# RWKV7 heads in a two-block kernel: one stationary tile of 128 columns for a chunk's outputs and next state, transposes in place of identity products, masked products in another order

## The chip, the cores and the metric

The kernel runs on one core of one Trainium2 chip. The metric is the device time of one execution in microseconds. A core has a tensor array (TensorE, PE in the rows; its weight loads are PEld), VectorE (DVE), ScalarE (ACT), GpSimd (POOL) and SyncE (SP), which issues the loads of the weights. Each engine takes its instructions in the order in which the program has them, and engines wait for one another by semaphores.

## What is computed

Two blocks on 256 tokens of 2048 features. The first has two layers; in each, four mixers of 512 columns (retention, HGRN2, mLSTM, RWKV7) run on one projection, then an output projection and a feed-forward part. The second block is one layer with sparse attention and a dilated mixture. The change lies in RWKV7 of the first block:

```python
def rwkv7_scan(r, log_w, k, v, kk, a):
    def step(state, inp):                      # state: 64 x 64 of each of 8 heads
        rt, lwt, kt, vt, kkt, at = inp
        state = (state * jnp.exp(lwt)[:, :, None, :]
                 - jnp.einsum('bhvk,bhk->bhv', state, kkt)[..., None] * (at * kkt)[:, :, None, :]
                 + vt[..., None] * kt[:, :, None, :])
        return state, jnp.einsum('bhvk,bhk->bhv', state, rt)

def rwkv7_group(p, ...):
    r, k, v, wd, ad, gd = split_cols(p + (token_shift(p) - p) * mu, RWKV_SPLIT)
    log_w = -RWKV_DECAY_SCALE * jax.nn.sigmoid(w0 + jnp.tanh(wd) @ w_up)
    a = jax.nn.sigmoid(a0 + ad @ a_up)
    kk = hs(k * k_k); kk = kk / norm(kk)
    k = k * (1.0 + (a - 1.0) * k_a)
    y = rwkv7_scan(hs(r), hs(log_w), hs(k), hs(v), kk, hs(a))
    ...                                        # norm of each head, bonus, gate
```

## The kernel before

**The stream.** All large matmuls run through `stream_a` (lines 147 to 152) or `stream_b` (195 to 197). A weight tile comes by DMA into `raw` (three buffers), ScalarE casts its high part to `hi` (line 104, four buffers), VectorE subtracts for `lo` (line 105), and the array multiplies both with activations that are split in the same way. A tile of 1024 columns is eight k-tiles; in the jobs of the mixers each k-tile takes three matmuls of 256 columns (lines 147, 148, 149), weights of 128 rows by 128 columns.

**RWKV7.** `rw_pair` handles two heads on 128 partitions, four times in each layer (`rw(0)` to `rw(3)` in `mixers`), so eight times in all. The 256 tokens are four chunks of 64, c = 2e + o. Pairs alternate between two sets of tiles (s = 0, 1) and two banks of PSUM each; `LI` and `TB` are one tile for all. The steps of a pair that matter here:

- line 968: the norm of kappa is spread over rows by two products with the identity (f32 products, two passes each in the trace);
- line 1000: [kappa; beta] x [alpha, rho], of each head the four chunks in a row, one head on partitions 0 to 63, the other on 64 to 127; line 1001 masks them into `W`, which has four slots of 64 columns for each head and chunk;
- lines 1018 to 1027: the inverse of (I + L) of 32 x 32 blocks in four rounds; line 1018 multiplies X with `LI` and, in the same 256 columns, with the identity; ScalarE negates the second half into `TB` (1023), VectorE transposes the first (1020), line 1025 multiplies again, lines 1026 and 1027 put the result into T and X;
- line 1038 transposes [kappa; beta]; lines 1044 and 1045 turn v and alpha by products with the identity, 64 columns of weights each;
- lines 1057 to 1083: the inverse of blocks of 64, X and T [X | alpha];
- line 1090: Ah^T times two slots of W, into two banks `g2[o]`; line 1096 makes `GT` and `PT` of them in four subtractions;
- lines 1103 and 1105: the state at the start of chunks 1 to 3, `W` (128 rows x 64 columns of weights) and `GT` (64 x 64), heads side by side; line 1106 scales it by the decay into `ST`;
- lines 1111 and 1113: the outputs of eight head-chunks from `W` (128 x 64) and `PT` (64 x 64); line 1115 copies them out.

Tile shapes are printed in the rows as rows*columns of weights, such as 64*64.

**What sets the order.** The program is written pair by pair; the tile framework's scheduler lays out each engine's queue by a simulated timeline. `K.first(100)` around `rw_pair` lets its instructions go before the last hundred traced ones, so the matmuls of a pair stand between those of the stream and of HGRN2 (`hg_pair`, lines 800 to 889).

Of the kernel before, what the change touches and what calls it, by code (L numbers as in the profile page):

```python
# [13 lines left out]
OP = mybir.AluOpType  # L14
AX = mybir.AxisListType
PSUM = bass.MemoryType.PSUM

D = 2048
# [10 lines left out]
class Squares:  # L29
    """Tiles of squares yet to be added up, and the bank of their means."""  # L30
# [5 lines left out]
class Core:  # L36
    """Pools, the weight stream and the norms that every part shares."""
# [19 lines left out]
    def g(self, i=0):  # L57
        """One bank of PSUM for the parts beside the stream, from one of their three pools."""
        return self.ps_g[i].tile([128, 512], F32, name="g", tag="g")

    def first(self, n):
        """What is traced in this goes before the n instructions traced last where it can, and beside what follows."""
        return self.tc.high_priority(offset=n)
# [26 lines left out]
    def prep(self, srcs, n, pool=False):  # L90
        """srcs: [128, n] each of DRAM in f32, or all in one [., 128, n] -> the two f32r parts of them all, side by side: hi + lo = w."""
# [16 lines left out]
    def stream_a(self, jobs, rhs, phases, feed=None, late=None, load=None, whole=None, bank=None):  # L108
        """jobs: [(weights [128, K], done, one)]: a tile of 128 columns each; rhs(k): [128, 512] = hi|lo of k-tile k.
        phases: lists of k-tiles (at most 8 in a row); within a phase k is outer over the jobs when there are several.  # L110
        A job with `one` gets the whole sum in its bank, as wide as the half of rhs; else it's the sum of the bank's two halves.
        load(phase), feed(phase): make what rhs gives of the phase; late(): what comes once the last of them are made.
        whole: [jobs, 128, K], the weights of all jobs; bank: where a single job's sum goes."""
# [43 lines left out]
    def stream_n(self, w, rhs, phases):  # L157
        """w: [128, K], only the first 64 of whose tile's 128 columns count; rhs, phases: as for stream_a. Returns their sums [64, 256]:
        the hi parts and the lo parts of the weights go through together."""
# [23 lines left out]
    def stream_b(self, w, nk, lhs, done):  # L183
        """w: [128, nk*512] of DRAM, 512 columns; lhs(k): [128, 512] = hi|lo; done(tt, bank) for the two tiles of tokens."""
# [16 lines left out]
    def half_sum(self, bank):  # L201
        """The two halves of a bank (of x's hi and lo) added, in SBUF."""
# [1880 lines left out]
```

## Time and profile before

| | |
|---|---|
| median of three runs | 3612.31 us (3606.8 to 3613.91) |
| span of the profiled execution, and its own time | 3606.8 us, 3606.8 us |
| tensor array busy (matmuls) | 3520.6 us, 98% |
| VectorE, ScalarE, GpSimd busy | 2484.1, 1746.3, 650.8 us |
| mean granted clock of the array | 0.990 |

The page gives busy time, the chain that ended last and the costliest groups. Matmul records are pipelined, so that the printed length of one overlaps the next; the time that one takes of the array is read from start to start in the timeline. RWKV7's pairs of the first layer lie at 50 to 380 us, those of the second at 1430 to 1780 us.

### The profile page before, as it was taken

Reading aid. Unit: us, or ns where it says so; the run is one execution under the profiler, and the core shown is the slowest. Engines: PE = TensorE matmul, PEld = TensorE weight load, DVE = VectorE, ACT = ScalarE, POOL = GpSimd, SP = SyncE. Lnnn points to the kernel's source line nnn. Section 1 sums busy time; section 2 is a strip of 40 time slices with the busy share of each in tenths; the row PEclk is TensorE's granted clock in tenths of the full one; section 3 lists DMA queues with packets and bytes.
Section 4 is the critical chain, followed back from the end, with each engine's and each line's share of the span. In section 5 each row is a group of like instructions: output and inputs, shape, how many; then the busy total and the mean of one; then the engine's idle time right before and its main releaser. Section 6 shows DMA issues by size and latency. Waiting matters only on the chain.

```text
span 3606.8 us, 62083 instructions
## 1 busy us (share of the span) xinstructions
PE 3520.6 (98%) x23920; PEld 3069.2 (85%) x23920; DVE 2484.1 (69%) x4464; ACT 1746.3 (48%) x2861; POOL 650.8 (18%) x822
## 2 busy tenths in 40 slices
PE   8999999999999999999999899999999999999998
PEld 8778888788888888877888788888888899988886
DVE  7676776777776557876786777777556866765555
ACT  5543454544444444634354544444444644654443
POOL 2122312311110003120420311111002213100001
PEclk9999999999999999999999999999999999999999
DMA  6335555677776664424455577777665555445554
GB/s 205 112 98 162 162 169 164 208 235 235 236 237 215 204 193 154 152 60 139 151 171 180 159 235 236 238 234 232 203 204 154 181 177 175 135 132 186 186 185 141
DMA packets 209369, 652.49 MB, mean 181 GB/s; under 512 B 24176, under 2 KB 27152, under 8 KB 209072
## 3 DMA queue, kind: packets, MB, share of 16 engines
q1 hardware_dynamic: 169664, 577.84, 51.1%
q10 hardware_dynamic: 39408, 70.67, 6.2%
q8 instruction: 188, 3.08, 0.3%
q14 instruction: 109, 0.89, 0.1%
HBM read 645.78 MB, written 2.65 MB: 180 GB/s over the span
## 4 chain that ended last, share of the span: by engine, by line
PE 89%; DVE 6%; issue 2%; ACT 1%; DMA 1%; POOL 0%; SPq 0%; DVEq 0%; ACTq 0%; POOLq 0%
PE s L151 34%; PE s L152 17%; PE s L147 5%; PE s L148 5%; PE s L149 5%; PE s L195 4%; PE s L196 4%; PE s L197 4%; DVE lo L105 1%; DVE h L314 1%; PE g L148 1%; PE g L149 1%; PE g L147 1%; DVE uq L300 1%; PE g L1018 1%
## 5 line engine op out<-in xcount | busy, mean ns | idle before, releaser
L105 DVE TENSOR_TENSOR lo<-raw,hi 128x1024 fp32r<-128x1024 f32 (+1 forms) x1101 | 1383.5, 1258 | 840.3 <-ACT hi L104 835.8
L104 ACT CAST hi<-raw 128x1024 fp32r<-128x1024 f32 (+1 forms) x1105 | 1142.3, 1036 | 1346.9 <-PE s L151 658.7
L151 PE MATMUL s<-uq,hi 128*128 128x512 f32 x3344 | 1176.2, 394 | 3.6 <-ACT hid L211 3.6
L152 PE MATMUL s<-uq,lo 128*128 128x256 f32 x3344 | 933.8, 279 | 0.0
L151 PEld LDWEIGHTS s<-uq,hi 128*128 128x128 f32 x3344 | 627.4, 188 | 154.1 <-ACT hid L211 4.2
L152 PEld LDWEIGHTS s<-uq,lo 128*128 128x128 f32 x3344 | 627.5, 188 | 0.2
L151 PE MATMUL s<-hid,hi 128*128 128x512 f32 x1320 | 466.5, 396 | 0.0
L147 PE MATMUL s<-uq,hi 128*128 128x256 f32 x1456 | 420.0, 288 | 5.1 <-ACT v L1423 4.0
L149 PE MATMUL s<-uq,lo 128*128 128x256 f32 x1456 | 419.4, 288 | 0.0
L148 PE MATMUL s<-uq,hi 128*128 128x256 f32 x1456 | 419.2, 288 | 0.0
L152 PE MATMUL s<-hid,lo 128*128 128x256 f32 x1320 | 372.2, 282 | 0.0
L151 PEld LDWEIGHTS s<-hid,hi 128*128 128x128 f32 x1320 | 248.0, 188 | 60.0
L147 PEld LDWEIGHTS s<-uq,hi 128*128 128x128 f32 x1456 | 276.8, 190 | 14.4 <-issue 6.3
L148 PEld LDWEIGHTS s<-uq,hi 128*128 128x128 f32 x1456 | 276.7, 190 | 7.6 <-issue 6.7
L149 PEld LDWEIGHTS s<-uq,lo 128*128 128x128 f32 x1456 | 276.9, 190 | 7.2 <-issue 6.2
L152 PEld LDWEIGHTS s<-hid,lo 128*128 128x128 f32 x1320 | 247.9, 188 | 0.0
L196 PE MATMUL s<-lo,uq 128*128 128x512 f32 x608 | 243.4, 401 | 2.1 <-DVE lo L105 2.1
L195 PE MATMUL s<-hi,uq 128*128 128x512 f32 x608 | 241.3, 402 | 1.4 <-DVE k L1252 0.7
L197 PE MATMUL s<-hi,uq 128*128 128x512 f32 x608 | 241.9, 400 | 0.0
L223 POOL TENSOR_TENSOR acc<-acc,sq 128x256 f32<-128x256 f32 x70 | 82.9, 1184 | 796.6 <-ACT sq L219 796.6
L373 POOL TENSOR_TENSOR gs<-e,R 128x256 f32<-128x256 f32 x88 | 80.0, 909 | 439.3 <-DVE e L206 404.2
L379 POOL TENSOR_TENSOR e<-e,R 128x256 f32<-128x256 f32 x88 | 79.4, 903 | 367.9 <-DVE e L206 367.9
(638 smaller groups left out, 5259.8 us busy)
## 6 DMA issues: line engine op xcount, KB each, us to landing
raw<-in_wg_dram SPq DMA_DIRECT2D x168, 512.0 KB, 4.6
raw<-in_wu_dram SPq DMA_DIRECT2D x168, 512.0 KB, 4.7
raw<-in_wd_dram SPq DMA_DIRECT2D x160, 512.0 KB, 3.7
raw<-in_wina_dram SPq DMA_DIRECT2D x154, 512.0 KB, 3.9
raw<-in_win2a_dram SPq DMA_DIRECT2D x130, 512.0 KB, 3.7
raw<-in_winb_dram SPq DMA_DIRECT2D x96, 512.0 KB, 3.8
raw<-in_wout_dram SPq DMA_DIRECT2D x96, 512.0 KB, 3.8
aw<-in_wada_dram ACTq DMA_DIRECT2D x192, 256.0 KB, 4.8
```

What stands on the lines that cost most here:

```text
L104: self.last_hi = nc.scalar.copy(hi[:, :n], raw[:, :n])
L105: self.last = (nc.gpsimd if pool else nc.vector).tensor_tensor(lo[:, :n], raw[:, :n], hi[:, :n].bitcast(F32), op=OP.subtract)
L147: nc.tensor.matmul(banks[i][:, 0:n], wh, x[:, 0:n], start=first, stop=False)
L148: nc.tensor.matmul(banks[i][:, 0:n], wh, x[:, n:2 * n], start=False, stop=False)
L149: nc.tensor.matmul(banks[i][:, 0:n], wl, x[:, 0:n], start=False, stop=last)
L151: nc.tensor.matmul(banks[i], wh, x, start=first, stop=False)
L152: nc.tensor.matmul(banks[i][:, 0:256], wl, x[:, 0:256], start=False, stop=last)
L195: nc.tensor.matmul(banks[tt], xh, wh, start=(k == 0), stop=False)
L196: nc.tensor.matmul(banks[tt], xh, wl, start=False, stop=False)
L197: nc.tensor.matmul(banks[tt], xl, wh, start=False, stop=(k == nk - 1))
L223: (nc.vector if i % 2 else nc.gpsimd).tensor_tensor(acc.parts[i % 2], acc.parts[i % 2], sq, op=OP.add)
L373: nc.gpsimd.tensor_tensor(g, e, rget(), op=OP.mult)
```

## The change

- `W` changes its slots: for even chunks [masked alpha | v, alpha | masked rho | kappa, beta], for odd ones the last two are exchanged, so that outputs and next state of a chunk come from one stationary tile of 128 columns, slots 2 and 3 together. The outputs of a chunk then stand on the partitions of its half of a token tile, the state on the others.
- `PG` holds P and G side by side, made in one subtraction from `RI`, a new tile for all pairs with rho and the identity; ScalarE copies rho into it from each pair's `AR`. The eight products of the old line 1090 go to one bank, in the order e, h, o.
- For each chunk two products with `W` (128 rows by 128 columns; 64 columns for the last) and two with `PG` (64 rows) add up in one bank, and one multiplication on 64 partitions makes the next state, with `dcs`, the decays laid out by ScalarE.
- Products with the identity become transposes: of the norm, of v and alpha (four of 128 x 128 instead of eight products with 64 columns), and of X in each round of the inverse.
- The masked products alternate between the heads, on two banks, and are masked in four operations instead of two.
- Docstrings and comments are gone, with blank lines in their place; in `rw_pair` lines move by 4 to 21, after it by 14.

The diff without those docstrings and comments:

```diff
         nc, K = self.nc, self.K
-        self.wLI, self.wTB = self.t([128, 5, 128], "wLI"), self.t([128, 4, 4, 32], "wTB")
-        nc.gpsimd.memset(self.wLI[:, 0:4], 0.0)
+        self.wLI, self.wTB = self.t([128, 4, 128], "wLI"), self.t([128, 4, 4, 32], "wTB")
+        nc.gpsimd.memset(self.wLI, 0.0)
         nc.gpsimd.memset(self.wTB, 0.0)
-        nc.gpsimd.tensor_copy(self.wLI[:, 4], K.ident)
+        self.wRI = self.t([128, 2, 2, 128], "wRI")
+        for o in range(2):
+            Q, i = slice(64 * o, 64 * o + 64), 64 - 64 * o
+            nc.gpsimd.tensor_copy(self.wRI[Q, :, :, i:i + 64].rearrange("p h e t -> p (h e) t"), self.cst["id64"][Q].unsqueeze(1).to_broadcast([64, 4, 64]))
     def rw_pair(self, p, r, k, v, wa, w, y, bon, ms):
...
         for tt in range(2):
-            nc.tensor.matmul(n[:, tt * 128:(tt + 1) * 128], ne[:, 2 * tt:2 * tt + 2].rearrange("p h d -> p (h d)"), K.ident, start=True, stop=True)
+            nc.tensor.transpose(n[:, tt * 128:(tt + 1) * 128], ne[:, 2 * tt:2 * tt + 2].rearrange("p h d -> p (h d)"), K.ident)
         k2 = self.t(A, "w3")
...
         KB = self.t([128, 2, 4, 64], "wKB")
-        AR = self.t([128, 4, 2, 64], f"wAR{s}")
+        AR = self.t([128, 2, 4, 64], f"wAR{s}")
         def ch(x):
...
         nc.gpsimd.tensor_tensor(KB[:, :, 0:4:3], ch(k2), ch(di), op=OP.mult)
-        nc.gpsimd.tensor_tensor(AR[:, :, 1], r.rearrange("p (c t) -> p c t", c=4), dc[:, :, 1:65], op=OP.mult)
+        nc.gpsimd.tensor_tensor(AR[:, 1], r.rearrange("p (c t) -> p c t", c=4), dc[:, :, 1:65], op=OP.mult)
         nc.vector.tensor_tensor(di, a, di, op=OP.mult)
...
         nc.vector.tensor_tensor(KB[:, :, 1:3], ch(kk), ch(di), op=OP.mult)
-        nc.vector.tensor_tensor(AR[:, :, 0], kk.rearrange("p (c t) -> p c t", c=4), dc[:, :, 0:64], op=OP.mult)
+        nc.vector.tensor_tensor(AR[:, 0], kk.rearrange("p (c t) -> p c t", c=4), dc[:, :, 0:64], op=OP.mult)
         KBf = KB.rearrange("p e o t -> p (e o t)")
...
         W = self.t([128, 2, 4, 256], f"wW{s}")
+        g2 = [self.g(), self.g()]
+        for c in range(4):
+            for h in range(2):
+                R = slice(64 * h, 64 * h + 64)
+                nc.tensor.matmul(g2[h][:, c * 128:(c + 1) * 128], KBf[R, c * 128:(c + 1) * 128], AR[R, :, c], start=True, stop=True)
         for h in range(2):
-            R = slice(64 * h, 64 * h + 64)
-            g = self.g()
-            for c in range(4):
-                nc.tensor.matmul(g[:, c * 128:(c + 1) * 128], KBf[R, c * 128:(c + 1) * 128], AR[R, c].rearrange("p a t -> p (a t)"), start=True, stop=True)
-            nc.vector.tensor_tensor(W[:, h].rearrange("p c (x t) -> p c x t", x=4)[:, :, 0:4:2], g.rearrange("p (c x t) -> p c x t", c=4, x=2),
-                                    cst["gmask"].rearrange("p (x t) -> p x t", x=2).unsqueeze(1).to_broadcast([128, 4, 2, 64]), op=OP.mult)
+            for o in range(2):
+                nc.vector.tensor_tensor(W[:, h].rearrange("p c (x t) -> p c x t", x=4)[:, o:4:2, 0:4:2 + o], g2[h].rearrange("p (c x t) -> p c x t", c=4, x=2)[:, o:4:2],
+                                        cst["gmask"].rearrange("p (x t) -> p x t", x=2).unsqueeze(1).to_broadcast([128, 2, 2, 64]), op=OP.mult)
+        RI = self.wRI
+        dcs = self.t([128, 4, 2], f"wdc{s}")
+        for h in range(2):
+            H = slice(64 * h, 64 * h + 64)
+            for o in range(2):
+                Q = slice(64 * o, 64 * o + 64)
+                nc.scalar.copy(RI[Q, h, :, 64 * o:64 * o + 64], AR[H, 1, o:4:2])
+                nc.scalar.copy(dcs[Q, :, h:h + 1], dc[H, :, 64:65])
         LI, TB = self.wLI, self.wTB
...
             g = self.g()
+            nc.tensor.transpose(g[:, 128:256], flat(X), K.ident)
             for u in range(4):
-                nc.tensor.matmul(g[32 * u:32 * u + 32, 0:256], X[:, u], LI[:, u:5:4 - u], start=True, stop=True)
+                nc.tensor.matmul(g[32 * u:32 * u + 32, 0:128], X[:, u], LI[:, u], start=True, stop=True)
             QT = self.t([128, 4, 32], "wQ")
-            nc.vector.transpose(flat(QT), g[:, 0:128])
             for u in range(4):
...
                 nc.scalar.mul(TB[B, :, u], g[B, 128:256].rearrange("p (i t) -> p i t", i=4), -1.0)
+            nc.vector.transpose(flat(QT), g[:, 0:128])
             for i in range(4):
...
             nc.tensor.transpose(g[:, c * 128:(c + 1) * 128], KBf[:, c * 128:(c + 1) * 128], K.ident)
-        nc.scalar.copy(W[:, :, :, 192:256].rearrange("p h c x -> p c h x"), g.rearrange("p (c h x) -> p c h x", c=4, h=2))
+        for o in range(2):
+            nc.scalar.copy(W[:, :, o:4:2, 192 - 64 * o:256 - 64 * o].rearrange("p h e x -> p e h x"), g.rearrange("p (e o h x) -> p e o h x", e=2, o=2, h=2)[:, :, o])
         g = self.g()
-        for c in range(4):
-            Q = slice(64 * (c % 2), 64 * (c % 2) + 64)
-            R = slice(64 - 64 * (c % 2), 128 - 64 * (c % 2))
-            nc.tensor.matmul(g[Q, c * 128:(c + 1) * 128], v[:, c * 64:c * 64 + 64], K.ident, start=True, stop=True)
-            nc.tensor.matmul(g[R, c * 128:(c + 1) * 128], AR[:, c, 0], K.ident, start=True, stop=True)
-        nc.scalar.copy(W[:, :, :, 64:128].rearrange("p h c x -> p c h x"), g.rearrange("p (c h x) -> p c h x", c=4, h=2))
+        for e in range(2):
+            nc.tensor.transpose(g[:, e * 128:(e + 1) * 128], v[:, e * 128:(e + 1) * 128], K.ident)
+        for e in range(2):
+            nc.tensor.transpose(g[:, 256 + e * 128:384 + e * 128], AR[:, 0, 2 * e:2 * e + 2].rearrange("p c t -> p (c t)"), K.ident)
+        for o in range(2):
+            Q, R = slice(64 * o, 64 * o + 64), slice(64 - 64 * o, 128 - 64 * o)
+            gv = g[Q].rearrange("p (i e h x) -> p i e h x", i=2, e=2, h=2)
+            nc.scalar.copy(W[Q, :, o:4:2, 64:128].rearrange("p h e x -> p e h x"), gv[:, 0])
+            nc.scalar.copy(W[R, :, o:4:2, 64:128].rearrange("p h e x -> p e h x"), gv[:, 1])
         TT = self.t([128, 4, 64], f"wTT{s}")
...
             nc.vector.tensor_scalar(W[R, :, o:4:2, 64:128], g[R].rearrange("p (h e x) -> p h e x", h=2, e=2)[:, :, :, 0:64], -1.0, None, op0=OP.mult)
-        g2 = [self.g(), self.g()]
+        g = self.g()
         for e in range(2):
-            for o in range(2):
-                for h in range(2):
-                    R = slice(64 - 64 * o, 128 - 64 * o)
-                    nc.tensor.matmul(g2[o][64 * h:64 * h + 64, e * 128:e * 128 + 128], Ah[R, 2 * h + e], W[R, h, 2 * e + o, 128:256], start=True, stop=True)
-        GT = self.t([128, 4, 64], f"wL{s}")
-        PT = self.t([128, 4, 64], f"wTT{s}")
-        for i, dst in ((1, GT), (0, PT)):
-            for o in range(2):
-                gv = g2[o][:, 0:256].rearrange("p (e t) -> p e t", e=2)[:, :, 64 * i:64 * i + 64]
-                nc.vector.tensor_tensor(dst[:, o:4:2], cst["id64"].unsqueeze(1).to_broadcast([128, 2, 64]) if i else AR[:, o:4:2, 1], gv, op=OP.subtract)
-        ST = self.t([128, 4, 64], f"wT{s}")
-        for c in range(3):
-            g = self.g()
             for h in range(2):
-                H = slice(64 * h, 64 * h + 64)
-                nc.tensor.matmul(g[H, 0:64], W[:, h, c, 192:256], W[:, h, c, 64:128], start=True, stop=(c == 0))
-                if c:
-                    nc.tensor.matmul(g[H, 0:64], GT[H, c], ST[H, c], start=False, stop=True)
-            nc.vector.tensor_scalar(ST[:, c + 1], g[:, 0:64], dc[:, c, 64:65], None, op0=OP.mult)
-        g2 = [self.g(), self.g()]
-        for h, e, o, c, u, R in units():
-            H = slice(64 * h, 64 * h + 64)
-            out = g2[h][64 * o:64 * o + 64, e * 64:e * 64 + 64]
-            nc.tensor.matmul(out, W[:, h, c, 128:192], W[:, h, c, 64:128], start=True, stop=(c == 0))
-            if c:
-                nc.tensor.matmul(out, PT[H, c], ST[H, c], start=False, stop=True)
-        for h in range(2):
-            nc.scalar.copy(y[:, :, p * 128 + h * 64:p * 128 + h * 64 + 64], g2[h][:, 0:128].rearrange("p (t x) -> p t x", t=2))
+                for o in range(2):
+                    Q, R = slice(64 * o, 64 * o + 64), slice(64 - 64 * o, 128 - 64 * o)
+                    n = (2 * h + e) * 128
+                    nc.tensor.matmul(g[Q, n:n + 128], Ah[R, 2 * h + e], W[R, h, 2 * e + o, 128:256], start=True, stop=True)
+        PG = self.t([128, 2, 2, 128], f"wAR{s}")
+        nc.vector.tensor_tensor(PG.rearrange("p h e x -> p (h e x)"), RI.rearrange("p h e x -> p (h e x)"), g, op=OP.subtract)
+        ST = self.t([128, 2, 2, 64], f"wT{s}")
+        g = self.g()
+        gv = g.rearrange("p (h c x) -> p h c x", h=2, c=4)
+        for c in range(4):
+            Q, R = slice(64 * (c % 2), 64 * (c % 2) + 64), slice(64 - 64 * (c % 2), 128 - 64 * (c % 2))
+            M = slice(64, 128) if c == 3 else slice(0, 128)
+            for h in range(2):
+                nc.tensor.matmul(gv[M, h, c], W[:, h, c, 128 + M.start:256], W[:, h, c, 64:128], start=(h == 0), stop=(c == 0 and h == 1))
+            for h in range(2 if c else 0):
+                nc.tensor.matmul(gv[M, h, c], PG[Q, h, c // 2, M.start:128], ST[Q, (c - 1) // 2, h], start=False, stop=(h == 1))
+            if c < 3:
+                nc.vector.tensor_tensor(ST[R, c // 2], gv[R, :, c], dcs[R, c].unsqueeze(2).to_broadcast([64, 2, 64]), op=OP.mult)
+        for o in range(2):
+            Q = slice(64 * o, 64 * o + 64)
+            nc.scalar.copy(y[Q, :, pc].rearrange("p e (h x) -> p h e x", h=2), gv[Q, :, o:4:2])
         yv = y[:, :, pc].rearrange("p t (h x) -> p t h x", h=2)
```

On the tensor array, the last of the states and the first outputs of the first layer's first pair, before. g is a bank of PSUM, wW0 is `W`, wT0 is `ST`, wL0 `GT`, wTT0 `PT`; L1025 is the inverse of the second pair, L148 the stream:

```order
L1105 MATMUL g_953<-wT0_942,wL0_936 64x64
L1103 MATMUL g_953<-wW0_758 64x64
L1105 MATMUL g_953<-wT0_942,wL0_936 64x64
L1111 MATMUL g_959<-wW0_758 64x64
L1025 MATMUL g_1211<-wTB_498,wQ_1216 32x128 x4
L1111 MATMUL g_959<-wW0_758 64x64
L1113 MATMUL g_959<-wT0_942,wTT0_937 64x64
```

On the tensor array, the second chunk of the first layer's third pair, now (wAR0_2725 is `PG`, L195 to L197 are the stream, L972 the norm of the fourth pair):

```order
L195 MATMUL s_3972<-hi_4011,uq_97 128x512
L1122 MATMUL g_2728<-wW0_2533 128x64 x2
L1124 MATMUL g_2728<-wT0_2727,wAR0_2725 128x64 x2
L972 MATMUL g_3638<-ident_82,w5_3660 128x128 x2
L195 MATMUL s_3973<-hi_3975,uq_96 128x512
```

Single products of `W` with `ST`'s partners in turns have become two wide products with `W`, then two with `PG`, and the outputs have no products of their own.

On ScalarE, behind the first pair's factors and among HGRN2's (hE, hS), where the first pair's PG is made, before:

```order
L858 COPY hS_1398<-g_1880 64x2x64
L831 ACTIVATE hE_1973<-hE_1973 128x256
L831 ACTIVATE hE_1996<-hE_1996 128x256
L104 CAST hi_2452<-raw_2451 128x1024
L833 ACTIVATE hE_2019<-hlf_1649 128x128
```

and now (wRI is `RI`, wAR1_1161 the second pair's `AR`, L104 a weight cast):

```order
L858 COPY hS_1392<-g_1874 64x2x64
L831 ACTIVATE hE_1990<-hE_1990 128x256
L1016 COPY wRI_501<-wAR1_1161 64x2x64 x4
L833 ACTIVATE hE_2013<-hlf_1643 128x128
L104 CAST hi_2446<-raw_2445 128x1024
```

The four copies into `RI` of the second pair stand ahead of a weight cast.

## Rows read from the trace of the kernel before

**Rows 1.** The page: busy time of the array, and the chain by engine.

```profile
PE 3520.6 (98%) x23920; PEld 3069.2 (85%) x23920; DVE 2484.1 (69%) x4464; ACT 1746.3 (48%) x2861; POOL 650.8 (18%) x822
...
PE 89%; DVE 6%; issue 2%; ACT 1%; DMA 1%; POOL 0%; SPq 0%; DVEq 0%; ACTq 0%; POOLq 0%
```

**Rows 2.** Table by stretch: from:to, length, busy PE PEld DVE ACT POOL, clock, DMA.

```profile
50.00:380.00 330.00, 327.31 (x3384) 273.43 (x3383) 236.42 (x587) 147.59 (x288) 71.84 (x116) 0.99 0.41 127
1430.00:1780.00 350.00, 342.51 (x3437) 281.40 (x3436) 256.29 (x637) 156.96 (x300) 78.02 (x131) 0.98 0.40 123
```

**Rows 3.** Waits, 50 to 380: who waited for whom, us, times, longest.

```profile
ACT hi L104 <- PE s L148: 65.2, 34, 4.3
```

**Rows 4.** Timeline of the array, outputs of pair one: start, length, instruction.

```profile
161.14 0.28 PE L147 MATMUL s<-uq,hi 128*128 128x256 f32 x1
161.35 0.33 PE L1105 MATMUL g<-wT,wL 64*64 64x64 f32 x2
161.61 0.33 PE L1103 MATMUL g<-wW 128*64 128x64 f32 x2
...
164.02 0.38 PE L148 MATMUL s<-uq,hi 128*128 128x256 f32 x1
164.24 0.28 PE L149 MATMUL s<-uq,lo 128*128 128x256 f32 x1
```

**Rows 5.** Timeline of the array: a run of L1090, a run of L1025.

```profile
201.78 0.65 PE L1090 MATMUL g<-wW,wP 64*64 64x128 f32 x8
202.36 0.39 PE L149 MATMUL s<-uq,lo 128*128 128x256 f32 x1
...
213.57 0.43 PE L1025 MATMUL g<-wTB,wQ 128*32 128x128 f32 x8
213.93 0.39 PE L149 MATMUL s<-uq,lo 128*128 128x256 f32 x1
```

**Rows 6.** Timeline of the array: a run of L1018.

```profile
92.74 0.64 PE L1018 MATMUL g<-wLI,wT 128*32 128x256 f32 x8
93.31 0.39 PE L148 MATMUL s<-uq,hi 128*128 128x256 f32 x1
```

**Rows 7.** Timeline of the array: the masked products of pair one.

```profile
73.45 1.71 PE L1000 MATMUL g<-wAR,wKB 64*128 64x128 f32 x16
75.09 0.61 PE L955 MATMUL g<-c_rwkv,w 128*128 128x2 f32 x4
```

**Rows 8.** Timeline of the array: identity products of pair three, first and next.

```profile
253.96 0.32 PE L1044 MATMUL g<-ident,v 128*64 128x128 f32 x1
...
254.98 0.37 PE L1057 MATMUL g<-wT,wW 32*32 32x32 f32 x10
```

**Rows 9.** Timeline of the array: four transposes, and what follows.

```profile
126.19 0.66 PE L1038 MATMUL g<-ident,wKB 128*128 128x128 f32 x4
126.60 0.37 PE L147 MATMUL s<-uq,hi 128*128 128x256 f32 x1
```

**Rows 10.** Timeline of the array, second block: products with 128 columns of weights.

```profile
3075.09 0.39 PE L1968 MATMUL g<-vsw,pt 128*128 128x64 f32 x2
3075.31 0.39 PE L1966 MATMUL g<-vsw,pt 128*128 128x64 f32 x2
```

**Rows 11.** Timeline of the array: eight products of L1078 in a row.

```profile
1609.32 1.09 PE L1078 MATMUL g<-wW,wTT 64*64 64x128 f32 x16
1610.34 0.50 PE L195 MATMUL s<-hi,uq 128*128 128x512 f32 x1
```

**Rows 12.** VectorE by line: count, busy us, mean ns, idle before.

```profile
L1001 DVE TENSOR_TENSOR wW<-g,c_rwkv 128x512 f32<-128x512 f32 x16 | 10.7, 685 | 7.0 <-PE g L1000 7.0
L1096 DVE TENSOR_TENSOR wL<-c_rwkv,g 128x128 f32<-128x128 f32 x16 | 4.5, 282 | 1.5 <-PE g L1090 1.5
```

**Rows 13.** ScalarE by line.

```profile
L1115 ACT COPY o<-g 128x128 f32<-128x128 f32 x16 | 4.2, 265 | 12.4 <-PE g L1113 12.3
```

**Rows 14.** Table by stretch: a stretch of half clock.

```profile
156.80:160.40 3.60, 3.60 (x18) 3.52 (x17) 2.64 (x9) 0.52 (x2) 0.60 (x2) 0.50 0.07 13
```

## The prediction

> **What bounds the kernel now.** I read the page first. The tensor array's matmul row is busy for 98% of the span and 89% of the chain that ended last is on it [rows 1]. Then the table by stretch: the RWKV7 pairs of the first layer run from 50 to 380 us, those of the second from 1430 to 1780. There the array is busy 327.3 of 330 and 342.5 of 350, VectorE 236 and 256, ScalarE 148 and 157 [rows 2]: the array waits 2.7 and 7.5 us, all told. Who waits for whom shows the same from the other end: ScalarE's casts of the weights stand still for 65 us behind matmuls that still hold their buffers [rows 3]. The stream of weights fills every hole, so what the small matmuls take from the array is taken from the end.
>
> So they are priced by the array's clockwork, from start to start in the timeline, not by the printed lengths, which overlap. A stream matmul of 256 columns starts 0.12 us after the one before. The last before a small run takes 0.21 and the first behind it 0.22 [rows 4], so **one visit of another tile shape costs 0.20 beside its own matmuls**. An f32 product is two passes (x2 in the rows). Where two shapes alternate, one product takes 0.255 [rows 4], though two passes of 64 columns alone would be far less: the change of shape is most of it.
>
> **The change part by part**, per pair of heads; there are eight pairs (four in each of two layers).
>
> *States and outputs (L1103 to L1113 before).* Before: 10 products for the states and 14 for the outputs. The states make 9 runs, the outputs 12 (two times two L1111 fall together), nearly each in another shape than its neighbour: 21 x 0.255 = 5.4, and some three visits to the stream, 0.6: 6.0. After: 8 products with W and 6 with PG. Six W products are 128 columns wide, in the stream's own shape, and such a product takes 0.22 with no end to pay [rows 10]: 1.3. Four PG products on 64 rows by 128 columns go two by two. No row has this shape with 64 moving columns. The lower bound for a run of two is one alternating product, 0.255 [rows 4]; the upper is two visits, one for each product, 2 x (0.255 + 0.20) = 0.91. I take 0.63, four passes at the 0.11 of [rows 10] plus the change of shape of 0.20, since both products use the same row half and cannot overlap; with the 0.20 of the visit 0.83, twice 1.7. The last chunk has two runs of two narrow products, 0.36 each with 0.20: 0.9. Sum 3.9, a gain of 2.1, **17 us for eight pairs**; 23 by the lower bound, and 11 if the PG runs cost the upper one and each product of the last chunk 0.255.
>
> *Inverse, L1018.* Four products with 256 columns take 0.57 [rows 6], the same shape with 128 columns 0.36 [rows 5]; the added transpose, a full-width single pass, 0.10 [rows 9]. Gain 0.10 to 0.11, 32 times: **3.3**. It is 0 if the transpose pays a change of shape of its own, 6.7 if it hides wholly.
>
> *Identity products.* Those of v and alpha, 16 passes, take 1.02 [rows 8] and about half a visit, 0.1; four transposes take 0.41 to 0.44 [rows 9]. Gain 0.68, **5.4**. The norm's two identity products become two transposes: two passes less of 0.11, **1.8**.
>
> *Masked products, L1000.* Sixteen passes take 1.64 [rows 7], because the two heads, on different row halves, overlap only in the middle. Sixteen passes that alternate between two quarters take 1.02 [rows 11]. Gain 0.62, **4.9**, or 0 if alternating does nothing.
>
> *G and P, L1090.* Before, two runs of eight passes at 0.58 [rows 5], two visits: 1.56. After, all eight products follow one another on two quarters in turn, like [rows 11]: 1.02 and one visit, 1.22. Some pairs had one visit already, so not 2.7 but **2** (bounds -3 and 2.7).
>
> Sum: 17 + 3.3 + 5.4 + 1.8 + 4.9 + 2 = **34 us** of the array. Two things are left out, of opposite sign. Visits of before are more broken than these clean ones, and in the two built orders the array changes shape 611 times before and 436 times after; by 175 x 0.20 = 35 for the shapes alone and the passes saved, the gain could be 41. Against that, the chains on VectorE and ScalarE stay as long as they were while the array's share between their steps shrinks by some 5%, and the 10 us of waits in the two stretches will grow, by 3 to 7. I set them against each other and keep 34.
>
> *Cover.* VectorE: four subtractions of 0.28 and two maskings of 0.69 [rows 12] become one subtraction as large as a masking, 0.69, and four maskings of half that size, by the two rows some 0.41 each (an estimate): 2.5 before, 2.3 after; the scalings of the state stay three. ScalarE gets twelve more copies a pair: four of rho into RI, four of the decay, four because the copies into W are cut by halves of the partitions. At the 0.27 of a copy of 128 columns [rows 13] that is 3.2 us, 13 in a stretch where it is busy 148 of 330. The array covers them, and a cast that comes 1 us late finds buffers ahead [rows 3]. If that cover were gone they would cost 26 us in all. No DMA is added or moved; GpSimd gets two small copies a layer before the first pair's products.
>
> *New wait.* RI is one tile for all pairs, so the copies of the next pair wait for the subtraction of the one before. Behind them in ScalarE's queue stand the HGRN factors and the next weight cast, and for that cast waits the stream. The built order has the copies late, between those of the HGRN states, where the subtraction should be near.
>
> **The rivals.** (a) *The chain takes back half.* Pairs depend on each other through LI, and VectorE is at 72 to 73% in both stretches [rows 2]; steps that were hidden behind array work show as waits. Against it: 10 us of waits in 680. Half of 34 lost: 3595. (b) *Nothing comes through*, the serial chain through VectorE sets both stretches and the array was only filled up to it: between nothing and 7 us, say 4: 3608. Against it speak the casts that wait for the array [rows 3]. (c) *One bank for two row halves.* The eight products of L1090 wrote two banks, one for each row half; now both halves write one. If they had to take turns, sixteen passes would take 16 x 0.11 = 1.76, not 1.02: 0.74 x 8 = 6 lost, 3584. Against it: the eight products of L1078 write one bank from both row halves and start sixteen passes in 1.02 [rows 11]. The Trainium skill has the rule (TensorEngine Tiling (Array Packing), Gotcha 1: PSUM Pressure): different row tiles go to different banks and cannot use the same one at once. By that rule the time is 3584, by the row 3578; the trace does not agree with it where the two write different partitions, and I go by the row. (d) *The clock.* The granted clock falls to 0.50 (1.2 GHz) in stretches such as 156.8 to 160.4 [rows 14], 3.6 us long, and each costs half its length, 1.8. One more for each pair: 14 lost, 3592. (e) *Slower: the RI wait holds the casts.* The four cast buffers hold 4 x 24 matmuls x 0.12 = 11.5 us of stream. If ScalarE stands at the copies longer than that, the array runs dry. There are six handovers (three a layer). To end slower by 7 us they must lose 41, 6.8 each, so it decides from a hold of 18 us; at 20, 6 x 8.5 = 51 are lost, 17 more than is gained: 3629. The copies' late place in the queue speaks against it.
>
> **How the numbers follow.** The profiled execution took 3606.8 us, all of it inside its span, and 34 less is 3572.8. It is the lowest of the three runs; the median, 3612.3, is 5.5 above, and a median is predicted: 3572.8 + 5.5 = **3578**; the rivals are counted from the median too. What a measurement of this kernel can tell from no change is 0.2%, 7 us. Chances: forecast 0.58 (gain 22 to 48, 3564 to 3590), (a) 0.18, (b) 0.06, (c) 0.06, (d) 0.06, (e) 0.04, and 0.02 for more than 48. Faster are the forecast, (a), (c), (d) and the last: 0.90; the same (b): 0.06; slower (e): 0.04. The range 3563 to 3601 holds the forecast, (c), (d) and most of (a).
>
> **What would show it.** Right: the W products at 0.22 each with the stream's next matmul 0.12 to 0.20 behind; masked products, sixteen passes in about 1.0; L1018's successor at 0.36 behind one transpose; waits of the array in the two stretches under 17 us together; each layer's mixers some 17 us shorter. Wrong: PG runs over 0.9, a run of the G and P products near 1.8 (c), waits of the array for VectorE in the stretches over 20 us (a, b), casts that wait behind RI copies (e), more half-clock stretches than before (d).

## The result, and the profile after

The changed kernel takes **3568.59 us** (median of 4 runs, 3567.99 to 3569.57), the kernel before, beside it, 3609.56 (3605.78 to 3613.91): ratio **0.9886, interval 0.9872 to 0.9900**, 41 us less. The profiled executions give the same: spans 3606.8 and 3565.9. A later set of runs on another chip gave 0.9890 (0.9875 to 0.9905). The forecast was 34 us less. All times here and below are of fast runs; one run, of narrow_again below, took 12941 us at a granted clock of 1.0 and is left out, its cause open.

The page after, in the order of [rows 1]:

```profile
PE 3481.8 (98%) x23680; PEld 3055.1 (86%) x23680; DVE 2483.3 (70%) x4456; ACT 1769.4 (50%) x2957; POOL 660.2 (19%) x824
...
PE 85%; DVE 8%; DMA 2%; ACT 2%; issue 2%; POOL 0%; ACTq 0%; SPq 0%; DVEq 0%; POOLq 0%
```

The array is busy 38.8 us less, and idle for 84.1 us of the span where it was 86.2. So the time was taken out of the array's work, and over the whole span none of it came back as waits. On the chain that ended last the array's share fell from 89% to 85%, and VectorE's rose from 6% to 8%. The table by stretch, with the columns of [rows 2]:

```profile
50.00:380.00 330.00, 324.02 (x3356) 278.37 (x3355) 255.35 (x618) 168.00 (x349) 88.41 (x132) 0.99 0.44 138
1430.00:1780.00 350.00, 342.20 (x3405) 294.02 (x3405) 273.64 (x655) 183.43 (x371) 84.34 (x128) 0.97 0.43 136
```

In the two stretches the waits are 6.0 and 7.8 us, where they were 2.7 and 7.5. The first masked product of the second layer starts 17.2 us earlier than before (1456.0 instead of 1473.2), as the forecast had it for one layer's mixers.

Where it went is read from the array's timeline. "Array time" below is worked out over all rows of it: for each instruction of a line the time from its start to the next one's start, less idle time, and what the last stream matmul ahead of a visit and the first behind it take over 0.118 us.

| part (lines before / after) | before | after | gain | forecast |
|---|---|---|---|---|
| states and outputs (1103 to 1113 / 1122, 1124) | 49.9 | 29.7 | 20.2 | 17 |
| inverse (1018 / 1032, 1034) | 27.8 | 22.7 | 5.1 | 3.3 |
| masked products (1000 / 1004) | 16.7 | 11.3 | 5.4 | 4.9 |
| v and alpha (1044, 1045 / 1059, 1061) | 8.9 | 4.2 | 4.7 | 5.4 |
| norm (968 / 972) | 4.2 | 2.3 | 1.9 | 1.8 |
| G and P (1090 / 1111) | 11.8 | 9.5 | 2.3 | 2 |
| sum | | | **39.6** | **34.4** |

A chunk of the chain after, timeline of the array (start, length, instruction):

```profile
1666.98 0.55 PE L1122 MATMUL g<-wW 128*128 128x64 f32 x4
1667.46 0.66 PE L1124 MATMUL g<-wT,wAR 64*128 64x64 f32 x4
1668.05 0.43 PE L1041 MATMUL g<-wTB,wQ 128*32 128x128 f32 x8
```

From start to start the two W products take 0.48, the two of PG, with the changes of shape at both sides, 0.59. Then the masked products (0.11 behind the stream's last, 1.09 for sixteen passes, where [rows 7] have 1.64), G and P, and a round of the inverse:

```profile
74.50 1.16 PE L1004 MATMUL g<-wAR,wKB 64*128 64x128 f32 x16
75.59 0.61 PE L959 MATMUL g<-c_rwkv,w 128*128 128x2 f32 x4
...
1605.58 1.09 PE L1111 MATMUL g<-wW,wP 64*64 64x128 f32 x16
1606.60 0.33 PE L1032 MATMUL g<-ident,wT 128*128 128x128 f32 x1
...
1671.97 0.28 PE L147 MATMUL s<-uq,hi 128*128 128x256 f32 x1
1672.08 0.27 PE L1032 MATMUL g<-ident,wT 128*128 128x128 f32 x1
1672.29 0.43 PE L1034 MATMUL g<-wLI,wT 128*32 128x128 f32 x8
1672.64 0.39 PE L148 MATMUL s<-uq,hi 128*128 128x256 f32 x1
```

G and P: sixteen passes in 1.02. A round of the inverse: 0.35 behind a transpose, which takes 0.21.

### The profile page after: what moved, and what is told of

The parts are those of the page before. It is cut to its first block, busy times and chain, and to the rows that moved or that the text cites. A ratio compares the mean times of both kernels' runs of the same rounds, so it can differ in the third digit from the quotient of the medians.

```text
span 3565.9 us, 61722 instructions
## 1 busy us (share of the span) xinstructions
PE 3481.8 (98%) x23680; PEld 3055.1 (86%) x23680; DVE 2483.3 (70%) x4456; ACT 1769.4 (50%) x2957; POOL 660.2 (19%) x824
## 4 chain that ended last, share of the span: by engine, by line
PE 85%; DVE 8%; DMA 2%; ACT 2%; issue 2%; POOL 0%; ACTq 0%; SPq 0%; DVEq 0%; POOLq 0%
PE s L151 34%; PE s L152 17%; PE s L147 5%; PE s L149 5%; PE s L148 5%; PE s L195 4%; PE s L196 3%; PE s L197 3%; DVE lo L105 2%; DVE h L314 1%; ACT hi L104 1%; DMA raw<-in_wina_dram 1%; PE g L148 1%; PE g L149 1%; DVE uq L300 1%
## 5 line engine op out<-in xcount | busy, mean ns | idle before, releaser
L104 ACT CAST hi<-raw 128x1024 fp32r<-128x1024 f32 (+1 forms) x1105 | 1141.6, 1035 | 1275.5 <-PE s L151 676.1
L148 PE MATMUL s<-uq,hi 128*128 128x256 f32 x1456 | 417.7, 287 | 0.0
L148 PEld LDWEIGHTS s<-uq,hi 128*128 128x128 f32 x1456 | 275.4, 189 | 5.9 <-issue 4.8
L195 PE MATMUL s<-hi,uq 128*128 128x512 f32 x608 | 242.8, 406 | 0.6 <-ACT vo L1867 0.4
L197 PE MATMUL s<-hi,uq 128*128 128x512 f32 x608 | 243.1, 401 | 0.0
```

Source lines behind the costliest of these rows:

```text
L104: self.last_hi = nc.scalar.copy(hi[:, :n], raw[:, :n])
L148: nc.tensor.matmul(banks[i][:, 0:n], wh, x[:, n:2 * n], start=False, stop=False)
L195: nc.tensor.matmul(banks[tt], xh, wh, start=(k == 0), stop=False)
L197: nc.tensor.matmul(banks[tt], xl, wh, start=False, stop=(k == nk - 1))
```

## The experiments

The theory (T1 in the expectations): the array never runs dry, so its time from start to start is the time; what costs in the small products is the change between tile shapes, and the parts add up. Against it: the number of products or the wide tile (W), the latency of the chains (L), the added ScalarE work (S).

One thing is needed to read differences of 5 us. Within one kernel the time follows the mean granted clock of the run: of the five runs of a_inv, one took 3576.58 us at 0.987, one 3568.34 at 0.990 and one 3560.03 at 0.992. Over the 100 runs of this section one line with a level for each kernel and chip fits with 2.8 us (plus or minus 0.4) for each 0.001 of clock. The last column is each kernel's time on that line at 0.990, with its 95% interval; on it the kernel before is at 3607 to 3610 on the three chips. The kernel after ran on one of the three (with a_mix, a_both and narrow_again); where the others are compared with it, that difference between chips stays in.

| kernel | median us | ratio to before, interval | array time of the part changed | at clock 0.990 |
|---|---|---|---|---|
| after, again | 3571.1 | 0.9890 (0.9875, 0.9905) | chain 30.3 | 3566.4 (2.8) |
| b_group | 3587.9 | 0.9936 (0.9918, 0.9954) | chain 49.9 to 33.0 | 3590.8 (2.2) |
| b_alt | 3602.5 | 0.9973 (0.9960, 0.9986) | masked 16.7 to 10.4 | 3602.5 (1.6) |
| a_mix | 3579.2 | 0.9913 (0.9898, 0.9927) | chain 29.7 to 36.0 | 3573.9 (2.9) |
| a_narrow | 3565.1 | 0.9864 (0.9847, 0.9881) | chain 29.7 to 27.0 | 3563.1 (2.4) |
| narrow_again (three runs) | 3562.3 | 0.9873 (0.9854, 0.9893) | chain to 27.7 | 3559.6 (3.2) |
| a_wide | 3563.1 | 0.9863 (0.9845, 0.9882) | chain 29.7 to 28.2 | 3563.6 (2.4) |
| a_both | 3565.0 | 0.9871 (0.9856, 0.9885) | chain 29.7 to 23.9 | 3559.4 (2.8) |
| a_ident | 3578.3 | 0.9921 (0.9904, 0.9938) | identity and norm 6.5 to 14.3 | 3572.5 (2.5) |
| a_inv | 3568.3 | 0.9883 (0.9865, 0.9902) | inverse 22.7 to 25.2 | 3567.6 (2.4) |
| a_load | 3580.2 | 0.9925 (0.9910, 0.9940) | transposes of KB 4.6 to 22.6 | 3579.7 (2.2) |
| a_acts | 3568.8 | 0.9892 (0.9876, 0.9908) | none | 3567.5 (2.5) |

The kernel after once more is the first row:

> The kernel after, unchanged, on the chip and beside the runs of the three kernels sent with it, so that differences of 5 us between variants of it can be judged. All theories: 3565 to 3572 us.

**b_group: the order alone, without the wide tile.**

```diff
-                if c:
-                    nc.tensor.matmul(g[H, 0:64], GT[H, c], ST[H, c], start=False, stop=True)
+            for h in range(2 if c else 0):
+                H = slice(64 * h, 64 * h + 64)
+                nc.tensor.matmul(g[H, 0:64], GT[H, c], ST[H, c], start=False, stop=True)
```

and in the same way for the outputs, four products with `W` and then those with `PT`, for e = 0 and e = 1.

> The kernel before (3609.6 us) with the same products, 64 columns wide, in the state and output chain; only their order is changed: the products of W of both heads first, then those of GT or PT, so a pair of heads has about 16 changes between the 128-row and the 64-row shape fewer per pair. Theory T1 (the cost of the chain is the end of each run of products of one shape, some 0.2 us each time, on an array that never stops): 3589 us, 20 to 21 less, nearly all that the change's own chain gave (its products went from 49.9 to 29.7 us of array time). Rival W (the gain came from the tile of 128 stationary columns, that is from half as many products): no change, 3606 to 3613 us. Rival L (the chain's latency was the cost, the array's time is covered): no change or up to 5 us more, since the first product of a state now waits behind more work.

3588 us: 18 to 23 of the 41 us come from the order of products that stayed as they were. The outputs of one pair, timeline of the array:

```profile
1686.80 0.34 PE L1112 MATMUL g<-wW 128*64 128x64 f32 x4
1687.07 0.33 PE L1116 MATMUL g<-wT,wTT 64*64 64x64 f32 x2
1687.32 0.34 PE L1112 MATMUL g<-wW 128*64 128x64 f32 x4
1687.59 0.34 PE L1116 MATMUL g<-wT,wTT 64*64 64x64 f32 x6
1687.86 0.38 PE L149 MATMUL s<-uq,lo 128*128 128x256 f32 x1
```

Four passes take 0.27 and six 0.27, hardly more than two passes did between changes of shape in [rows 4], 0.26. From row to row of the trace the shape changes 541 times instead of 617, 76 less (the expectation's 16 for each pair, 128, was a miscount): 16.9 us of array time over 76 is 0.22 us for one change. That price holds more than the change: the grouped products also stand on different halves of the columns, and four or six passes cost no more than two. W and L fall.

**a_mix: the reverse, on the kernel after.** Each head's PG product stands right behind its W product:

```diff
             for h in range(2):
                 nc.tensor.matmul(gv[M, h, c], W[:, h, c, 128 + M.start:256], ...)
-            for h in range(2 if c else 0):
-                nc.tensor.matmul(gv[M, h, c], PG[Q, h, c // 2, M.start:128], ...)
+                if c:
+                    nc.tensor.matmul(gv[M, h, c], PG[Q, h, c // 2, M.start:128], ...)
```

> The kernel after (3568.6 us) with the same products of 128 columns in the chain, in another order: each head's product of PG right behind its product of W, instead of both of W first. That is two changes of shape more for each of three chunks of a pair, 48 in all. T1: regrouping the kernel before took 128 changes out and 16.9 us of array time, 0.13 us each; a run of 4 passes of PG's shape takes 0.585 us against 0.36 where no shape changes, so 0.13 to 0.25 us each: 3575 to 3581 us, 6 to 12 more. Rival W (the width of the tile gave the gain): no change.

3579 us beside 3571 of the kernel after: 7.5 to 8 more, as T1 said. A chunk, the same as the one above:

```profile
1669.93 0.33 PE L1122 MATMUL g<-wW 128*128 128x64 f32 x2
1670.19 0.43 PE L1124 MATMUL g<-wT,wAR 64*128 64x64 f32 x2
1670.56 0.43 PE L1122 MATMUL g<-wW 128*128 128x64 f32 x2
1670.92 0.43 PE L1124 MATMUL g<-wT,wAR 64*128 64x64 f32 x2
1671.28 0.33 PE L1032 MATMUL g<-ident,wT 128*128 128x128 f32 x1
```

1.35 instead of 1.07 for the same four products; three chunks of eight pairs by 0.28 make 6.7, and the whole chain's array time rose by 6.3. The shape changes 486 times instead of 442: 0.14 us for each of 44. Here the two products of a run stand on the same rows and columns of the array, so the new order changes the shapes alone, and this is the cleaner price of a change.

**a_narrow and narrow_again: the wide tile in halves.** Each product of the chain with 128 stationary columns becomes two with 64; the order of W and PG stays.

```diff
+            parts = [slice(a, a + 64) for a in (0, 64)][M.start // 64:]
             for h in range(2):
-                nc.tensor.matmul(gv[M, h, c], W[:, h, c, 128 + M.start:256], ...)
+                for m in parts:
+                    nc.tensor.matmul(gv[m, h, c], W[:, h, c, 128 + m.start:128 + m.stop], ...)
```

> The kernel after (3568.6 us) with each product of 128 stationary columns in the chain split into two of 64 columns, in the same grouped order, so that there are as many products as in the kernel before but as few changes of shape as after. T1: two halves stand on different columns of the array and the shape changes no more often than before the split; 3565 to 3572 us. Rival W (what was gained is the number of products): about 42 products of 4 passes come back, some 10 us, 3577 to 3580 us.

> The kernel after with the chain's products in halves of 64 columns once more, unchanged from its first run, beside the kernel after on the same chip. T1, with the array time of the first run (chain 27.0 us against 29.7, run of 8 passes 0.38 us against 0.48 to 0.59 for 4 passes at 128 columns): 2 to 5 us below the kernel after. Rival N (the first run's 3565 us was chance): equal to it within 1 us.

```profile
1670.76 0.45 PE L1124 MATMUL g<-wW 128*64 128x64 f32 x8
1671.14 0.45 PE L1127 MATMUL g<-wT,wAR 64*64 64x64 f32 x8
1671.52 0.33 PE L1032 MATMUL g<-ident,wT 128*128 128x128 f32 x1
```

The same chunk in 0.76 instead of 1.07, with twice the products: eight passes on two column halves in turn take 0.38, four passes at full width 0.48 and 0.59. Both are below the kernel after: a_narrow by 3.5 to 6 us at the median (beside the first and the later runs of that kernel) and 3 at equal clock, narrow_again, on the same chip, by 8.8 and 7. So W is not only refuted: the tile of 128 columns, taken by itself, costs a little. Nor is it the count of changes that decides here: the halves have another shape than the stream, and the array changes shape 473 times, 31 more than in the kernel after. What the two halves gain by overlapping is more than that. The intervals of the ratios still overlap with that of the kernel after, so the size in time is open; that the chain takes less of the array is in both traces.

**a_wide and a_both: no change of shape inside a chunk.** PG over all 128 rows, with the states beside rows of zeros in a tile of their own; a_both also has the halves.

```diff
+        self.wST = self.t([128, 2, 2, 64], "wST")
+        nc.gpsimd.memset(self.wST, 0.0)
...
-                nc.tensor.matmul(gv[M, h, c], PG[Q, h, c // 2, M.start:128], ST[Q, (c - 1) // 2, h], ...)
+                nc.tensor.matmul(gv[:, h, c], PG[:, h, c // 2], ST[:, (c - 1) % 2, h], ...)
```

> The kernel after (3568.6 us) with the products of PG over all 128 rows: the states lie in a tile whose other 64 rows are zeros, written once, so that PG's products have the shape of W's and the chain has no change of shape inside a chunk; for chunk 3 the whole 128 columns are formed too. More work for the array by columns times rows, the same number of products. T1: the three groups of a pair lose the end of the run in each, 0.2 to 0.25 us, 24 groups: 3562 to 3564 us, 5 to 6 less. Rival W (products and passes count): no change, 3567 to 3570 us. Rival L (the latency of the chain counts): no change.

> The kernel after with both variants at once: PG's products over all 128 rows (states beside zeros), and every product of the chain in halves of 64 columns; all of a chunk's products then have one shape. T1: 24 changes of shape less than with the halves alone, 0.13 us each, 3 us: 3559 to 3563 us, 6 to 9 less than the kernel after. Rival W: slower than the kernel after by 5 to 10 us, for the number of products doubles.

A chunk of a_wide and one of a_both:

```profile
1709.10 0.55 PE L1123 MATMUL g<-wW 128*128 128x64 f32 x4
1709.49 0.61 PE L1125 MATMUL g<-wST,wAR 128*128 128x64 f32 x4
1709.91 0.36 PE L148 MATMUL s<-uq,hi 128*128 128x256 f32 x1
```

```profile
1718.04 0.45 PE L1125 MATMUL g<-wW 128*64 128x64 f32 x8
1718.32 0.40 PE L1128 MATMUL g<-wST,wAR 128*64 128x64 f32 x8
1718.65 0.43 PE L651 MATMUL g<-v,rs 128*128 128x64 f32 x2
```

0.81 and 0.61 instead of 1.07: the zeros cost less than a change of shape. a_wide's time came as expected, but not its array time: the chain fell by only 1.5 us where 5 to 6 were expected, though the shape changes 403 times instead of 442. Eight of the 24 chunks are last ones and grew to 128 columns (0.81, from 0.75); sixteen by 0.26 less eight by 0.06 would still be 3.7. The rest lies in chunks that stand broken among other work, which no run separates. So its 2.8 us at equal clock, with an interval of 4 to either side, stay open. a_both has the shortest chain of all (23.9), with 466 changes of shape, more than the kernel after, and is **7 us below the kernel after** at equal clock, with an interval of 4 to either side (at the median 3565.0, above the 3559 to 3563 expected, and 6 below); its ratio, 0.9871 against 0.9890 on the same chip, has intervals that overlap, so which of the variants is best is not settled.

**b_alt: the masked products alone, on the kernel before.**

```diff
+        g2 = [self.g(), self.g()]
+        for c in range(4):
+            for h in range(2):
+                R = slice(64 * h, 64 * h + 64)
+                nc.tensor.matmul(g2[h][:, c * 128:(c + 1) * 128], KBf[R, ...], AR[R, c]..., start=True, stop=True)
         for h in range(2):
-            R = slice(64 * h, 64 * h + 64)
-            g = self.g()
-            for c in range(4):
-                nc.tensor.matmul(g[:, c * 128:(c + 1) * 128], KBf[R, ...], AR[R, c]..., start=True, stop=True)
```

> The kernel before (3609.6 us) with only the masked products changed: the two heads alternate from chunk to chunk, each on its own bank, nothing else. T1: the run of 16 passes falls from 1.64 to 1.09 us, 8 pairs by 0.55 and the lone passes with it: 3604 to 3605 us, 5 less. Rival W (only the wide tile gave the gain): no change. Rival H (the second bank that is held longer stalls other work on PSUM): slower by 2 to 8 us.

```profile
1531.82 1.16 PE L1000 MATMUL g<-wAR,wKB 64*128 64x128 f32 x16
1532.91 0.68 PE L1073 MATMUL g<-wW 64*64 64x64 f32 x16
```

The run of sixteen passes is 1.09, as after; 9.5 us less at the median and 6 at equal clock, with 6.3 of array time.

**a_ident and a_inv: one part undone.** a_ident puts the identity products back (v and alpha as eight of 64 columns, now v's four ahead of alpha's, and the norm's two); a_inv the inverse's product with 256 columns:

```diff
-            nc.tensor.transpose(g[:, 128:256], flat(X), K.ident)
             for u in range(4):
-                nc.tensor.matmul(g[32 * u:32 * u + 32, 0:128], X[:, u], LI[:, u], ...)
+                nc.tensor.matmul(g[32 * u:32 * u + 32, 0:256], X[:, u], LI[:, u:5:4 - u], ...)
```

> The kernel after (3568.6 us) with the products by the identity put back for v, alpha and the norm's factors, all else as changed. T1 (parts add up, array time is the path): the array time of these lines goes from 4.2 + 2.3 back to 8.9 + 4.2 us: 3575 us, 6.7 more (5 to 8). Rival L (something other than array time sets the end): no change, 3567 to 3570 us.

> The kernel after (3568.6 us) with the inverse's product and its identity product in one of 256 columns, as before the change, all else as changed. T1: 5.2 us of array time come back (22.65 to 27.8): 3574 us, 4 to 6 more. Rival L (the inverse is a chain through VectorE, and its array time is hidden): no change, 3567 to 3570 us.

a_ident: 6 us more at equal clock (9.7 at the median), 7.8 of array time; here are the identity products of one pair, 1.02 in all, where the four transposes of the kernel after take 0.36:

```profile
1637.52 0.66 PE L1060 MATMUL g<-ident,v 128*64 128x128 f32 x8
1638.01 0.61 PE L1063 MATMUL g<-ident,wAR 128*64 128x128 f32 x8
1638.54 0.38 PE L149 MATMUL s<-uq,lo 128*128 128x256 f32 x1
```

```profile
1689.04 0.38 PE L1059 MATMUL g<-ident,v 128*128 128x128 f32 x2
1689.26 0.38 PE L1061 MATMUL g<-ident,wAR 128*128 128x128 f32 x2
1689.40 0.36 PE L148 MATMUL s<-uq,hi 128*128 128x256 f32 x1
```

a_inv **stays open in the times**: 1 us more at equal clock, with an interval of 4 to either side. Its array time rose by 2.5 us, half of what was expected; a run with 256 columns is 0.57 again, and the transpose before it gone:

```profile
1691.26 0.28 PE L148 MATMUL s<-uq,hi 128*128 128x256 f32 x1
1691.46 0.64 PE L1034 MATMUL g<-wLI,wT 128*32 128x256 f32 x8
1692.03 0.61 PE L1050 MATMUL g<-c_rwkv,w 128*128 128x2 f32 x4
```

The run alone saves almost nothing: 0.57 against 0.21 for the transpose and 0.35 for the products, 0.56. What is saved stands ahead of it: the transpose has the stream's own shape, so the stream's matmul before it takes 0.11 where it takes 0.20 before the narrow products.

**a_load and a_acts: more work for one engine.** a_load puts `for _ in range(6):` around the four transposes of KB; a_acts adds twelve copies behind those into `RI` and `dcs`:

```diff
+        spare = self.t([128, 2, 64], "wsp")
+        for _ in range(12):
+            nc.scalar.copy(spare, AR[:, 1, 0:4:2])
```

> The kernel after (3568.6 us) with five more rounds of the four transposes of KB in each of the 8 pairs, into the same bank, ahead of the real ones: 160 transposes whose results nothing reads, each 0.11 us. T1 (PE's time is the path one to one): 17.5 us more, 3586 us. Rival L (the array has holes there that take it): 0 to 8 us more.

> The kernel after (3568.6 us) with twelve more copies on ScalarE in each of the 8 pairs (128x128 each, about 0.27 us), into a tile that nothing reads, right behind the copies that the change adds there: 25 us of ScalarE in all. T1 (the change's 23 us of added ScalarE work are covered): 3568 to 3572 us. Rival S (the added ScalarE copies are on the path, and ate a part of the gain): up to 26 us more, 3585 to 3595 us.

a_load: 12 to 14 us more by the ratios, 13.3 at equal clock, for 18.0 us of array time (thirteen transposes below take 1.34). Array work arrives in the time, if not quite whole (17.5 were expected): in the profile the array is busy 16.3 us more and idle 1.9 less.

```profile
1701.25 1.58 PE L1055 MATMUL g<-ident,wKB 128*128 128x128 f32 x13
1702.59 0.36 PE L147 MATMUL s<-uq,hi 128*128 128x256 f32 x1
```

a_acts: 1 us more at equal clock, with an interval of 4 to either side, though the 96 copies took ScalarE 29 us; in the profile the array's idle time is 89.8 us, 84.1 and 86.1 in the two profiles of the kernel after. Rival S, up to 26 us, falls. The line of the copies, by its own view (count, least, median and greatest ns, first and last start, form):

```profile
L1020 ACT COPY wsp<-wAR x96: 281/299/313, 64.0 to 1640.3; 128x128 f32<-128x128 f32 x96
```

## Why the forecast was right, point by point

- *What bounds it.* Right: a_load costs time, a_acts none that can be told from scatter, and the array's total idle time did not grow.
- *States and outputs, 17.* 20.2: the W products, 0.48 for two, and the PG run, 0.59 where 0.63 was taken, are near their terms. The missing 3 us come from both sides: 49.9 is 1.9 more than the eight visits priced at 6.0, and 29.7 is 1.5 less than the eight at 3.9. But the prediction read the saving as one of the wide tile, and the runs say otherwise: b_group gets 16.9 without it, and halving the tile makes the chain shorter.
- *The step that was mis-sized* is the balance behind the sum. Up to 7 us more from broken visits were set against new waits of 3 to 7. The parts gave 39.6 instead of 34.4, 3.2 of the 5.2 more in the chain and 1.8 in the inverse; how much of it is broken visits, no run separates. The waits rose by 3.6 us in the two stretches (13.8 from 10.2) and fell elsewhere, so in total nothing stood against it. The count of changed shapes gave 41, the measured gain, but that is partly luck: at a_mix's price of 0.14 the 175 changes (617 to 442 in the traces) would make 24.5, and a_narrow and a_both have more changes than the kernel after and a shorter chain.
- *Inverse, 3.3.* Before to after 5.1, but a_inv says 2.5 for the edit alone, and its time leaves even that open. The transpose was taken at 0.10 and takes 0.21, with the change of shape behind it; it gives back 0.09 at the stream's matmul ahead, which the prediction did not count. What makes up the rest of the 5.1 is not shown.
- *Identity products, norm, masked products, G and P.* 5.4, 1.8, 4.9 and 2 were 4.7, 1.9, 5.4 and 2.3; a_ident and b_alt show three of them in the time; G and P has no run of its own. At equal clock b_group, b_alt, a_ident and a_inv make 18 + 6 + 6 + 1 = 31 us; the rest of the 41 has no run behind it.
- *Cover and rivals.* (a) and (b) did not come: no growth in total idle time. (c) is refuted by the row of L1111, 1.02 for sixteen passes on one bank from both row halves. The rule in the Trainium skill (TensorEngine Tiling (Array Packing), Gotcha 1: PSUM Pressure), that row tiles cannot use one bank at once, would make it 1.76; the trace does not agree where they write different partitions. (d) The profile of the kernel after spends 80 us at a granted clock of 0.50 where that of the kernel before spends 74; at half their length that is 3 us. No effect of the change is seen in it: the other kernels' profiles have 66 to 96, and over the runs the mean clock moved both ways, to 0.990 from 0.989 for a_narrow and a_wide on one chip, to 0.988 from 0.990 for the kernel after on another. The stretch of [rows 14] was read too short: it began at 153.5 and lasted 6.8 us, so one more like it would cost 3.4 and not 1.8. (e) ScalarE did wait for the subtraction, but little. The copies of rho into `RI`, what ScalarE's idle time before them ended with (us, times):

```profile
L1016 ACT COPY wRI<-wAR x32: 288/297/299, 64.0 to 1659.4; 64x128 f32<-64x128 f32 x32
...
  DVE wAR L1113: 4.6, 3
```

and casts still wait for the array in the first stretch, not the array for them (as in [rows 3]):

```profile
ACT hi L104 <- PE s L148: 43.6, 26, 4.4
```

The stretch of half clock in the kernel before, table by stretch:

```profile
153.50:160.30 6.80, 6.80 (x57) 5.34 (x52) 4.15 (x16) 1.50 (x6) 0.50 (x2) 0.50 0.05 10
```

## What to carry to other kernels

Where the array is full, price small products from start to start and look at the changes of tile shape in the order as issued: here each was 0.14 us where nothing else changed, and sorting the same products by shape gave most of what the new tile gave. The count alone does not rank kernels, for overlap can be worth more: alternate the halves or quarters of the array within a run, rows in the masked products and columns in the chain. Full-width zeros or a transpose can be cheaper than the narrower shape that saves them.

## What the runs showed that was not expected

Products on the two column halves overlap: eight passes of 128 rows by 64 columns took 0.38 us and four 0.27, while four passes of 128 by 128 took 0.48. The Trainium skill says that different tiles can work in parallel and that a change of mode drains the array (TensorEngine Tiling (Array Packing), Key Properties); the trace agrees with both and adds a price for the second, 0.14 us by a_mix (6.3 us over 44 changes more).

Most of the scatter of a kernel's runs goes with the clock. Two stretches of a_inv's profile, table by stretch:

```profile
1526.00:1532.90 6.90, 6.47 (x70) 5.85 (x68) 6.66 (x15) 3.51 (x10) 4.77 (x8) 1.00 0.27 78
1533.00:1546.70 13.70, 13.70 (x152) 11.39 (x151) 10.08 (x31) 3.64 (x11) 3.54 (x6) 0.50 0.14 39
```

The granted clock falls to 0.50, the lower of the two levels (1.2 GHz), in the middle of a pair of heads; in the 6.9 us before it fell the array was busy for 6.47. The kernel after has such stretches at other places (1513.2 to 1520.0). They fall differently in each run, and at 2.8 us for 0.001 of mean clock they are as large as several parts of this change.
